# V kept per head pair as it lies in SBUF, its loads spread over SyncE's queue, and the last pair's transfers put in another order

## The chip, the cores and the metric

The kernel runs on one core of a Trainium2 chip: TensorE (PE), VectorE (DVE), ScalarE (ACT), GpSimd (POOL) and SyncE (SP), and 16 DMA engines that all of them feed. The metric is the device time of one execution in microseconds (us), the median of several runs; lower is better.

## The reference

One decoder layer in float32, 2048 tokens by 1024 features. One input projection feeds two branches; their gated, normed outputs are concatenated and go through one output projection, with a residual and a layer norm.

```python
# attention: 16 heads of 64, for each dilation in (1, 4, 16):
scores = einsum(q, k) + alibi            # keys: current and previous block of 128 on each
p = exp(scores - lse)                    # of the `dilation` residue subsequences
o[d] = einsum(p, v)
# the three dilations are merged by their log-sum-exp weights, gated by silu(z), RMS-normed
# Mamba-2 branch: causal conv, chunked state-space scan (chunks of 128), gate, RMS norm
u = concat(att, ssm)                     # 2048 features
out = layer_norm(alpha * x + u @ w_out)
```

## The kernel before

**Stage 1** (to about 1142 us) computes the input projection, the convolution and the scan, all in PE-bound blocks. Weights are split in two fp32r parts, and three matmuls stand for one product. V goes to a DRAM tensor `d_v[0]` in token order, 1024 features a token. `copy_v` then makes `d_v[1]`, the order that dilation 4 reads: 32 DRAM-to-DRAM transfers of 256 KB on POOL's queue, 16 in about 357 to 560 us and 16 in 864 to 1130 us, in pieces of 2 KB. In the second phase POOL's queue also reloads prepared weights (`w<-d_wc`, L237).

**Stage 2** (about 1142 to 1613 us) is attention, in 8 head pairs. A pair has 24 units, named (d, qd, half): d counts the dilations in the order 16, 4, 1, qd the four groups of blocks, half the head. PE runs a software pipeline: the scores of one unit (L947), the transposes of the unit two before (L976), the values of the unit three before (L1002). DVE adds bias and takes maxima (L953), ACT does the exps (L962), DVE copies the transposed probabilities out of PSUM (L978). For a unit, V is read through two tiles: `v`, and `vs`, which is V shifted by half a block.

What one pair leaves is merged during the next one: the softmax statistics are transposed (tile `st`, into `sT`), stored in `d_st`, gathered back in another order (`cm`, L1061), turned into weights in three steps (`weights`, on DVE, POOL and ACT), stored in `d_wd` and read back three times, once for each dilation, as a row broadcast over 64 partitions (`broadcast`, tile `wb`, L1089). `combine(0)` to `combine(5)` multiply (L1111), add (L1115) and gate them into the pair's u. u lies in a `wb` buffer until `keep_u` (L1096) stores it in `d_ua`; a broadcast starts with a memset of one column on DVE (L1087), which takes the buffer over. All pairs but the last one are merged on POOL; the last one on DVE.

**Stage 3** (about 1596 to 2002 us) is the output projection, in items of 24 matmuls (L1201 to L1203): block of tokens n, branch br (1 the scan, 0 attention), half of the features. The order is blocks 0 to 3 of the scan branch first (items 0 to 7), then block 0 of the attention branch (items 8 and 9), and so on. An item needs its block fetched (`fetch_raw`), split in two fp32r parts (`split`: cast L1167, subtraction L1169), its squares (L1174), and 8 weight tiles W[0..7] or W[8..15] (`load_w`, L1142). Item 8 is the first to need the last pair's u.

Code is written in the order of one list, and PE, DVE, ACT and POOL run in that order in stages 2 and 3. SP's queue was ordered by a scheduler in stage 3. Loads hang on the unit at which they are issued: `STEPS` gives the unit's combine step and a load on POOL's queue, `LOADS` the weight loads of the last pair. A queue issues in order: a transfer that has to wait holds up those behind it.

Of the kernel before, what the change touches and what calls it, by code (L numbers as in the profile page):

```python
# [17 lines left out]
D = 1024  # L18
NR = 16
# [9 lines left out]
def hybrid_layer(ctx, tc, xb, xc, w52, wv, wdt, convw, convb, dtb, alog, dskp, gcol, wout,  # L29
# [18 lines left out]
    d_v = [dtile(f"d_v{d}", [16, 128, D]) for d in range(2)]  # L48
# [10 lines left out]
    d_ua = dtile("d_ua", [16, 128, 7, 128])  # L59
# [11 lines left out]
    with ExitStack() as c1:  # L71
# [281 lines left out]
        def fin_v(s, p):  # L353
            def f(ci, q, b, e):
                for x in range(2):
                    nc.sync.dma_start(dap(d_v[0], 4 * (8 * p + 4 * q + 2 * b + x) * D + 512 * s + 256 * ci,
                                          [[64 * D, 32], [D, 4], [1, 256]]), e[:, 256 * x:256 * x + 256])
            return f
# [188 lines left out]
        def copy_v(s, b):  # L547

            o = (b % 4 * 512 + b // 4 * 16) * D + 512 * s
            nc.gpsimd.dma_start(dap(d_v[1], b * 128 * D + 512 * s, [[16 * D, 8], [D, 16], [1, 512]]),  # L550
                                dap(d_v[0], o, [[64 * D, 8], [D, 16], [1, 512]]))
# [298 lines left out]
    with ExitStack() as c2:  # L850
# [29 lines left out]
        def load_v(A, x, d, queue=nc.gpsimd):  # L880

            o, t, c0 = int(x == "vs"), io.tile([128, 16, 128], F32, name=x, bufs=3), A["pr"] * 128
            A[x][d] = t
            if d == 0:
                for j in range(4):
                    nc.gpsimd.dma_start(t[j:128:4], dap(d_v[0], j * D + c0, [[64 * D, 32], [4 * D, 16], [1, 128]]))
            else:
                queue.dma_start(t[:, 0:16 - o], dap(d_v[d % 2], 64 * o * D + c0,
                                                        [[D, 128], [128 * D, 16 - o], [1, 128]]))
# [193 lines left out]
        def broadcast(A, d):  # L1083

            wb = A["w", d] = cm_.tile([128, NR, NJ], F32, name="wb", bufs=3)
# [9 lines left out]
        def keep_u(A, queue):  # L1095
            queue.dma_start(dap(d_ua, A["pr"] * 128, [[7 * 128, 128], [128 * 7 * 128, 16], [1, 128]]),  # L1096
                            A["u"].rearrange("p (n t) -> p n t", t=128))

        def combine(A, k):
# [50 lines left out]
        def fetch_raw(n, br, u=None):  # L1150
# [5 lines left out]
            else:  # L1156
                queue.dma_start(u[:, 0:7], d_ua[n])
# [21 lines left out]
        def residual(n):  # L1179
            o = O[n] = os_[n // 2][:, n % 2 * D:n % 2 * D + D] if n < 4 else O.pop(n - 4)  # L1180
            (nc.scalar if n < 4 else nc.sync).dma_start(o, xc[n * 128:(n + 1) * 128, :])
# [38 lines left out]
        def norm(n):  # L1220
# [10 lines left out]
            if n == 15:  # L1231
                for s in (slice(0, 512), slice(512, D)):
# [13 lines left out]
                 (1, 1, 0): (1, "k", 1), (1, 2, 0): (2, "v", 1, 0), (1, 3, 0): (3, None, 0), (2, 0, 0): (None, "v", 1, 1),  # L1246
                 (2, 1, 0): (4, "vs", 1, 1), (2, 2, 0): (5, None, 0)}
        LOADS = {(1, 0, 0): ((8, None, "k_0"),), (1, 1, 0): ((9, None, "q_0"),), (1, 2, 0): ((11, None, "vs"),),
                 (1, 3, 0): ((12, 0, "q_1"), (13, 0, "v")), (2, 1, 0): ((10, None, "ex"),),
                 (2, 2, 0): ((14, 0, "v"), (15, 0, "vs"))}  # L1250
# [4 lines left out]
        with tc.manual_schedule(engines={E.PE, E.DVE, E.Activation, E.Pool, E.SP}):  # L1255
            for i in range(len(todo) + TA + 1):
# [27 lines left out]
                if i > TA:  # L1284
# [32 lines left out]
                    if pr == 7 and at in ((2, 0, 1), (2, 1, 0)):  # L1317
                        split(0, 1, slice(4 * qd, 4 * qd + 4), (0,))
                    if pr == 7 and at == (2, 1, 0):
                        split(0, 1, parts=(1,))  # L1320
# [11 lines left out]
                    if pr < 7:  # L1332
                        continue
                    for e, hf, name in LOADS.get(at, ()):
                        load_w(e, hf, name)
# [159 lines left out]
```

## Time and profile before

| what | value |
|---|---|
| runs | 2010.32, 2006.55, 2009.21 us; median 2009.21 |
| profiled execution | 2003.82 us, span 2002.0 us, clock 0.991 |
| busy: PE, DVE, ACT, POOL | 1945.7, 1275.8, 1120.0, 998.3 us |
| DMA | 447.67 MB, mean 224 GB/s |

The profile is one execution, 5.4 us under the median. PE is busy 97% of the span, so what is left to find lies in its few waits. "PE S L1203 <- DVE num L1169: 12.0, 1, 12.0" reads: PE, about to run line 1203 into tile S, waited for DVE's line 1169 on tile num, 12.0 us in total, once, 12.0 at the longest. An "issue" wait is one for which the profile shows no releaser.

### The profile page before, as it was taken

How to read it: one execution, taken by the hardware profiler on the slowest of the kernel's cores; microseconds unless marked ns; L12 is line 12 of the kernel's file. 1: busy time of each engine (PE TensorE's matmuls, PEld its weight loads, DVE VectorE, ACT ScalarE, POOL GpSimd, SP SyncE). 2: the span in 40 equal slices, each digit the busy share in tenths (PEclk: the TensorE clock that was granted, in tenths of full speed). 3: DMA queues.
4: the chain of work that ended last, by engine and by line, in shares of the span. 5: the costliest groups of instructions: out<-in, count | busy, mean ns of one | idle time of the engine just before them, and what ended most of it. 6: DMA issues, size and time to landing. Idle time of an engine off the chain costs nothing.

```text
span 2002.0 us, 42714 instructions
## 1 busy us (share of the span) xinstructions
PE 1945.7 (97%) x16008; PEld 1588.2 (79%) x16008; DVE 1275.8 (64%) x3204; ACT 1120.0 (56%) x3036; POOL 998.3 (50%) x877
## 2 busy tenths in 40 slices
PE   8999999999999999999999999999999888999998
PEld 7888899888888888988888877777777666888886
DVE  7655376887766655644454388888887736655553
ACT  5454343566556774456566488988888732322220
POOL 0366514666556667155565343676776622432221
PEclk9999999999999999999999999999999998999999
DMA  6788676566787876888888766888888988332210
GB/s 270 236 284 293 213 280 227 159 195 190 237 306 266 279 245 239 312 269 256 272 277 259 256 228 165 229 244 235 252 238 254 265 242 260 134 102 92 92 61 32
DMA packets 260656, 447.67 MB, mean 224 GB/s; under 512 B 44785, under 2 KB 146673, under 8 KB 249057
## 3 DMA queue, kind: packets, MB, share of 16 engines
q1 hardware_dynamic: 170912, 205.39, 32.2%
q0 software_dynamic: 39088, 142.54, 21.6%
q10 hardware_dynamic: 50448, 97.01, 15.7%
q8 instruction: 126, 2.06, 0.4%
q14 instruction: 82, 0.66, 0.1%
HBM read 301.85 MB, written 151.39 MB: 226 GB/s over the span
## 4 chain that ended last, share of the span: by engine, by line
PE 85%; DVE 5%; DMA 4%; ACT 3%; issue 2%; POOL 1%; SPq 0%; ACTq 0%; DVEq 0%; POOLq 0%
PE pp L260 13%; PE pp L264 13%; PE pp L262 13%; PE N L1002 7%; PE S L947 6%; PE T L976 5%; PE pp L309 4%; PE S L1201 4%; PE S L1203 4%; PE S L1202 3%; PE ss L309 2%; PE T L1201 2%; PE T L1203 2%; PE T L1202 2%; PE ss L627 2%
## 5 line engine op out<-in xcount | busy, mean ns | idle before, releaser
L217 POOL TENSOR_TENSOR w<-wr,w 128x512 fp32r<-128x512 f32 x217 | 285.6, 1327 | 268.2 <-ACT w L216 184.0
L962 ACT ACTIVATE P<-P,st 128x192 f32<-128x192 f32 (+1 forms) x768 | 323.4, 423 | 59.9 <-DVE st L953 55.4
L252 ACT COPY ev<-pp 128x512 f32<-128x512 f32 x200 | 117.1, 587 | 315.3 <-PE pp L264 281.5
L953 DVE CUSTOM_DVE_ANT_0 P<-S,tb 128x192 f32<-128x192 f32 (+1 forms) x768 | 205.8, 324 | 53.6 <-PE S L947 44.1
L272 DVE TENSOR_TENSOR ev<-pp,ev 128x512 f32<-128x512 f32 x152 | 101.2, 686 | 140.6 <-PE pp L264 95.9
L216 ACT CAST w<-wr 128x512 fp32r<-128x512 f32 x224 | 134.1, 620 | 23.5 <-DVE wr L211 11.9
L962 ACT ACTIVATION_READ_ACCUMULATOR P<-P,st 128x1 f32 x768 | 145.0, 189 | 0.0
L1111 POOL TENSOR_TENSOR wb<-num,wb 128x2048 f32<-128x2048 f32 x21 | 95.7, 4558 | 93.7 <-DMA wb<-d_wd 90.2
L978 DVE COPY PT<-T 128x512 f32<-128x512 f32 x192 | 131.7, 686 | 3.8 <-PE T L976 3.8
L976 PE MATMUL T<-ident,P 128*128 128x128 f32 x768 | 127.3, 288 | 6.7 <-DVE PT L978 4.5
L1002 PE MATMUL N<-PT,v 128*64 128x64 f32 (+1 forms) x1536 | 124.5, 259 | 4.2 <-DVE PT L978 3.5
L976 PEld LDWEIGHTS T<-ident,P 128*128 128x128 f32 x768 | 81.3, 141 | 52.9 <-ACT P L962 16.8
L211 DVE TENSOR_TENSOR wr<-wr 128x512 f32<-128x512 f32 x128 | 112.2, 877 | 9.3 <-DMA wr<-w 5.9
L947 PE MATMUL S<-k,ex 64*64 64x192 f32 (+1 forms) x2048 | 108.8, 322 | 3.2 <-issue 3.2
L1002 PEld LDWEIGHTS N<-PT,v 128*64 128x64 f32 x1536 | 79.4, 138 | 38.3 <-issue 22.7
L459 DVE SCALAR_TENSOR_TENSOR ss<-U,cw,ss 128x512 f32<-128x512 f32 x144 | 106.0, 752 | 2.9 <-ACT ss L455 0.6
L1177 DVE TENSOR_REDUCE tb<-P 128x128 f32<-128x1024 f32 x30 | 60.2, 2006 | 45.1 <-ACT P L1174 21.1
L1239 POOL TENSOR_TENSOR k<-k,wb 128x1024 f32<-128x1024 f32 x8 | 25.8, 3225 | 122.0 <-DVE k L1238 122.0
L587 ACT ACTIVATE mt<-csb,wdr 128x128 f32<-128x128 f32 x256 | 78.9, 395 | 0.9 <-PE ss L627 0.8
L947 PEld LDWEIGHTS S<-k,ex 64*64 64x64 f32 x2048 | 66.4, 134 | 15.4 <-issue 8.9
L596 DVE TENSOR_TENSOR mt<-mt,ss 128x1024 f32<-128x1024 f32 x32 | 39.0, 1220 | 54.1 <-ACT mt L592 53.7
L260 PE MATMUL pp<-TT4h,w 128*128 128x512 f32 x176 | 69.6, 395 | 0.0
(493 smaller groups left out, 5991.1 us busy)
## 6 DMA issues: line engine op xcount, KB each, us to landing
wr<-w ACTq DMA_DIRECT2D x164, 256.0 KB
d_wc<-w SPq DMA_DIRECT2D x48, 512.0 KB
w<-d_wc POOLq DMA_DIRECT2D x48, 512.0 KB, 6.4
wb<-d_wd SPq DMA_DIRECT2D x48, 512.0 KB
d_wo<-wot POOLq DMA_DIRECT2D x32, 512.0 KB, 4.3
csb<-d_cs ACTq DMA_DIRECT2D x32, 512.0 KB
d_wv<-w SPq DMA_DIRECT2D x14, 1024.0 KB
w<-d_wv POOLq DMA_DIRECT2D x14, 1024.0 KB, 8.7
```

Source lines behind the costliest of these rows:

```text
L216: nc.scalar.copy(h, r)
L217: low.tensor_tensor(l, r, h.bitcast(F32), op=OP.subtract)
L260: nc.tensor.matmul(ps, w[:, 0, k], th[:, k], start=start and k == 0, stop=False, skip_group_check=not start)
L262: nc.tensor.matmul(ps, w[:, 0, k], tl[:, k], start=False, stop=False, skip_group_check=not start)
L264: nc.tensor.matmul(ps, w[:, 1, k], th[:, k], start=False, stop=(k == 3), skip_group_check=not start)
L309: nc.tensor.matmul(o, (th, tl)[j == 1][:, k, t], w[:, int(j == 2), k], start=start and r % 2 == k == j == 0, stop=(k == 3 and j == 2), ski ...
L947: nc.tensor.matmul(o, A["q"][d][64 * h:64 * h + 64, blk, 64 * a:64 * a + 64], kv, start=True, stop=True)
L953: nc.vector.tensor_tensor_reduce(P[:, h, cs], sp[h][:, cs], t, -0.125, 3.0e38, OP.add, OP.min, accum_out=stat(A, 0, d, h, blk))
L962: nc.scalar.activation(p, p, AF.Exp, bias=stat(A, 0, d, h, blk), scale=-1.0, accum_out=stat(A, 1, d, h, blk))
L976: nc.tensor.transpose(tp[:, h, i], P[:, h, 256 * i:256 * i + 128], ident)
L978: nc.vector.tensor_copy(pt, tp)
L1002: nc.tensor.matmul(o, l, r, start=start, stop=True, skip_group_check=True)
```

## The change

1. *V's layout.* `d_v[1]` goes. `d_vt[1]` and `d_vt[2]` hold V for dilations 4 and 1 by head pair, each as the [128, 2048] tile that SBUF takes. `copy_v` issues two transfers where it issued one, in pieces of 512 B. A load of `v` is then 128 rows of 8 KB, one of `vs` two halves of 64 rows of 7.5 KB.
2. *Where loads are issued.* `v` and `vs` of dilation 4 move from POOL's queue to SP's, at (0,0,0) and, for the next pair, (2,0,1); `v` of dilation 1 at (0,1,1) and `vs` at (1,1,1), where both were at (0,0,0). `keep_u` moves from (1,0,0) to (0,0,1), and writes rows of 8 KB; `fetch_raw` of the attention branch now reads 7 pieces of 512 B for each partition.
3. *The last pair and the passage to stage 3.* The fetch of blocks 0 and 1 of the scan branch, the loads of W[10], W[11], W[14], W[15] and of z for pair 7, and `split(0, 1)` stand at other units. After item 0 SP gets: weights' store, broadcast 0, two residuals, broadcasts 1 and 2, `keep_u` of pair 6, two residuals, all in program order. ACT's queue carries no transfers there any more. At item 2 only `combine(0)` stands, at item 3 the third block's `split`, then `combine(1)` to `combine(5)`.

The core of the diff:

```diff
+            nc.gpsimd.dma_start(dap(d_vt[1], t + n * 512, [[128, 4], [16 * 2048, 8], [2048, 16], [1, 128]]),
+                                dap(d_v, 16 * n * D + c, [[512 * D, 4], [64 * D, 8], [D, 16], [1, 128]]))
+            nc.gpsimd.dma_start(dap(d_vt[2], t + 32 * n * 2048, [[2048, 32], [128, 16], [1, 128]]),
+                                dap(d_v, 32 * n * D + c, [[D, 32], [128 * D, 16], [1, 128]]))
...
-                queue.dma_start(t[:, 0:16 - o], dap(d_v[d % 2], 64 * o * D + c0,
-                                                        [[D, 128], [128 * D, 16 - o], [1, 128]]))
+                queue.dma_start(t[0:64, 0:15], d_vt[d][A["pr"], 64:128, 0:15])
+                queue.dma_start(t[64:128, 0:15], d_vt[d][A["pr"], 0:64, 1:16])
...
-            queue.dma_start(dap(d_ua, A["pr"] * 128, [[7 * 128, 128], [128 * 7 * 128, 16], [1, 128]]),
-                            A["u"].rearrange("p (n t) -> p n t", t=128))
+            queue.dma_start(d_ua[A["pr"]], A["u"])
...
-                if last:
-                    broadcast(A, d)
...
-                 (1, 1, 0): (1, "k", 1), (1, 2, 0): (2, "v", 1, 0), (1, 3, 0): (3, None, 0), (2, 0, 0): (None, "v", 1, 1),
-                 (2, 1, 0): (4, "vs", 1, 1), (2, 2, 0): (5, None, 0)}
...
+                 (1, 1, 0): (1, "k", 1), (1, 2, 0): (2, None, 0), (1, 3, 0): (3, None, 0), (2, 0, 0): (None, "v", 1, 0),
+                 (2, 1, 0): (4, None, 0), (2, 2, 0): (5, None, 0)}
...
+                 (1, 3, 0): ((12, 0, "q_1"), (13, 0, "v")), (2, 0, 0): ((11, None, "num"), (14, 0, "v"), (15, 0, "vs")),
+                 (2, 1, 0): ((10, None, "ex"),)}
...
+                    if at == (0, 0, 0) and pr:
+                        load_v(pairs[pr], "v", 1, nc.sync)
+                    if at == (0, 1, 1) and pr:
                         load_v(pairs[pr], "v", 2, nc.sync)
-                        load_v(pairs[pr], "vs", 2, nc.sync)
-                    if pr > 1 and at == (1, 0, 0):
+                    if pr > 1 and at == (0, 0, 1):
                         keep_u(pairs[pr - 2], nc.sync)
+                    if pr and at == (1, 1, 1):
+                        load_v(pairs[pr], "vs", 2, nc.sync)
+                    if pr < 7 and at == (2, 0, 1):
+                        load_v(pairs[pr + 1], "vs", 1, nc.sync)
...
                 if i == 2:
-                    for j in range(2):
-                        scaled(j)
-                    add(*adds.pop(0))
-                    add(*adds.pop(0))
-                    for j in range(3):
-                        combine(A, j)
+                    combine(A, 0)
                     load_w(0, 0, "num")
...
+                        broadcast(A, 0)
                         for n in range(2):
                             residual(n)
+                        broadcast(A, 1)
+                        broadcast(A, 2)
+                        keep_u(pairs[6], nc.sync)
+                        for n in range(2, 4):
+                            residual(n)
```

SP's queue around the merge of one pair in a steady pair, before: `d_st` and `cm` are the statistics' store and gather, the two loads named d_v are V's for the pair itself, `d_wd` the weights' store, `wb<-d_wd` a broadcast (x2, one for each head), `d_ua` u's store, `tb` a table.

```order
L1055 DMA d_st_115<-sT 16x16x8 x4
L1061 DMA cm<-d_st_115 128x6x32
L888 DMA v<-d_v_84 128x16x128
L888 DMA vs<-d_v_84 128x15x128
L878 DMA tb_15636<-tabs 128x2x320
L1081 DMA d_wd_123<-cm 128x3x32
L1089 DMA wb<-d_wd_123 64x2048 x2
L1096 DMA d_ua<-wb 128x16x128
```

And the same place after:

```order
L1061 DMA d_st_115<-sT 16x16x8 x4
L1067 DMA cm<-d_st_115 128x6x32
L892 DMA v<-d_vt_85 128x2048
L1103 DMA d_ua<-wb 128x2048
L892 DMA v<-d_vt_86 128x2048
L882 DMA tb_14582<-tabs 128x2x320
L1087 DMA d_wd_123<-cm 128x3x32
L1096 DMA wb<-d_wd_123 64x2048 x4
L894 DMA vs<-d_vt_86 64x1920
L895 DMA vs<-d_vt_86 64x1920
```

u's store now stands ahead of the weights' store and the broadcasts, and the load of vs behind two of the broadcasts.

DVE in the passage to stage 3, before, from the products of the first items on: L1111 and L1115 are the last pair's combine, L1169 and L1177 split and square sums of the third block (then of others), L1218 adds an item's result.

```order
L1218 SCALAR_TENSOR_TENSOR k<-S,st,k 128x512 x2
L1111 TENSOR_TENSOR wb<-num,wb 128x2048 x2
L1115 TENSOR_TENSOR wb<-wb 128x2048
L1169 TENSOR_TENSOR num<-P,num 128x1024
L1177 TENSOR_REDUCE tb_19949<-P 128x128
L1111 TENSOR_TENSOR wb<-num,wb 128x2048
```

And after:

```order
L1115 TENSOR_TENSOR wb<-num,wb 128x2048
L1173 TENSOR_TENSOR vs<-P,vs 128x1024
L1222 SCALAR_TENSOR_TENSOR k<-S,st,k 128x512 x2
L1115 TENSOR_TENSOR wb<-num,wb 128x2048
L1119 TENSOR_TENSOR wb<-wb 128x2048
L1181 TENSOR_REDUCE tb_20003<-P 128x128
```

The third block's subtraction stands behind one combine step, where it stood behind three.

PE at the end of attention, before: L1002 are values, L1201 to L1203 the product of item 0, whose weight tiles are k (W[8]), q (W[9]), ex (W[10]) and so on.

```order
L1002 MATMUL N_19728<-PC,v 64x64 x2
L1002 MATMUL N_19727<-PT,v 64x64 x2
L1002 MATMUL N_19727<-PT,vs 64x64 x2
L1002 MATMUL N_19728<-PT,vs 64x64 x2
L1002 MATMUL N_19728<-PT,v 64x64 x2
L1201 MATMUL S<-ex,num 128x512
L1202 MATMUL S<-ex,num 128x512
```

And after, where the whole product stands ahead of the last units' values (L1008):

```order
L1008 MATMUL N_19715<-PC,v 64x64 x2
L982 MATMUL T<-ident,P 128x128 x4
L1207 MATMUL S<-q,vs 128x512
L1205 MATMUL S<-ex,vs 128x512
L1206 MATMUL S<-ex,vs 128x512
L1207 MATMUL S<-ex,vs 128x512
L1205 MATMUL S<-num,vs 128x512
```

The product's matmuls from ex (W10) on moved from behind these values to ahead of the last two units' values and the transpose of st.

More of the change, by code (lines that the diff above doesn't have):

```diff
@@ L47, in hybrid_layer @@
     d_za = [dtile(f"d_za{i}", [128, S]) for i in range(8)]
-    d_v = [dtile(f"d_v{d}", [16, 128, D]) for d in range(2)]
+    d_v = dtile("d_v", [16, 128, D])
+    d_vt = {d: dtile(f"d_vt{d}", [8, 128, 16, 128]) for d in (1, 2)}
     d_wc = dtile("d_wc", [12, 7, 128, 1024])
@@ L1083, in broadcast @@
         def broadcast(A, d):
-            wb = A["w", d] = cm_.tile([128, NR, NJ], F32, name="wb", bufs=3)
+            pool, name = (io, "v") if A["pr"] == 7 and d == 2 else (cm_, "wb")
+            wb = A["w", d] = pool.tile([128, NR, NJ], F32, name=name, bufs=3)
             if d and A["pr"] < 7:
@@ L1316, in hybrid_layer @@
                         load_z(pairs[pr - 1])
[L1317 to L1320, printed above, removed]
+                    if pr < 7 and at == (2, 0, 1):
+                        load_v(pairs[pr + 1], "vs", 1, nc.sync)
+                    if pr == 7:
+                        if at == (1, 0, 0):
+                            X = big("ex", F32)
+                            for j in range(2):
+                                fetch_raw(j, 1, X[:, j * D:j * D + D])
+                        if at == (1, 2, 0):
+                            free.append(big("vs"))
+                        if at == (2, 0, 0):
+                            zt7 = cm_.tile([128, NR, NJ], F32, name="num", bufs=6)
+                            nc.sync.dma_start(f2(zt7), d_za[7])
+                        for e, hf, name in LOADS.get(at, ()):
+                            load_w(e, hf, name)
+                        if at == (2, 0, 0):
+                            free.append(big("num"))
+                        if at in ((1, 2, 1), (1, 3, 0)):
+                            split(0, 1, slice(4 - 4 * half, 8 - 4 * half), (0,))
+                        if at == (2, 0, 0):
+                            split(0, 1, parts=(1,))
+                        if at in ((2, 2, 1), (2, 3, 0)):
+                            fetch_raw(qd, 1)
                     if at in STEPS:
@@ L1331, in hybrid_layer @@
                         permute(pairs[pr + 1], 1)
[L1332 to L1335, printed above, removed]
-                    if at == (2, 0, 0):
-                        zt7 = cm_.tile([128, NR, NJ], F32, name="num", bufs=6)
-                        free += [big("num"), big("num")]
-                    if at == (1, 2, 0):
-                        X = big("ex", F32)
-                        for j in range(2):
-                            fetch_raw(j, 1, X[:, j * D:j * D + D])
-        with tc.manual_schedule(engines={E.PE, E.DVE, E.Activation, E.Pool}):
+        with tc.manual_schedule(engines={E.PE, E.DVE, E.Activation, E.Pool, E.SP}):
             A = pairs[7]
@@ L1347, in hybrid_layer @@
             free.append(big("ex"))
-            fetch_raw(2, 1)
             squares(0, 1)
@@ L1386, in hybrid_layer @@
                         os_.insert(0, big("k_1", F32))
+                        broadcast(A, 0)
                         for n in range(2):
                             residual(n)
+                        broadcast(A, 1)
[3 more added lines that the diff above has]
+                            residual(n)
+                    if i == 3:
+                        for n in range(2):
+                            scaled(n)
+                        add(*adds.pop(0))
+                        add(*adds.pop(0))
+                        combine(A, 1)
+                        load_w(1, 0, "num")
+                        combine(A, 2)
                     squares(*ops[j])
-                    if i == 0:
-                        keep_u(pairs[6], nc.scalar)
-                        nc.scalar.dma_start(f2(zt7), d_za[7])
                     for m in (j + 2,) if 4 < j < 30 else ():
@@ L1406, in hybrid_layer @@
                 if i == 4:
-                    for e, name in enumerate(("num", "vs", "v", "wb", "num", "wb", "num")):
-                        load_w(1 + e, 0, name)
+                    for e, name in enumerate(("wb", "wb", "num", "wb", "num")):
+                        load_w(3 + e, 0, name)
                         if e == 2:
```

32 lines of the change are left out of this document (14 added, 18 removed).

## The prediction

> **What bounds the kernel now.** I read the page first, then a table of stretches, then the waits of PE, and then, where PE waits, the chain and the timelines around it.
>
> ```profile
> PE 1945.7 (97%) x16008; PEld 1588.2 (79%) x16008; DVE 1275.8 (64%) x3204; ACT 1120.0 (56%) x3036; POOL 998.3 (50%) x877
> ```
>
> The span is 2002.0 us, so PE stands still for 56 us in all: no edit that leaves PE's own instructions alone can bring more than that, plus what a slow clock costs. The next table (columns: window, its length, then PE, PEld, DVE, ACT, POOL busy, clock, DMA share, GB/s) says where those 56 us lie.
>
> ```profile
> 860.00:1140.00 280.00, 280.00 (x1574) 233.40 (x1573) 131.54 (x247) 163.64 (x336) 157.34 (x165) 1.00 0.82 264
> ...
> 1180.00:1540.00 360.00, 346.48 (x6653) 260.21 (x6651) 302.11 (x1531) 309.74 (x1384) 229.71 (x184) 1.00 0.79 224
> 1540.00:1590.00 50.00, 47.24 (x900) 35.14 (x900) 41.48 (x213) 42.83 (x195) 32.41 (x27) 1.00 0.85 233
> 1590.00:1613.00 23.00, 18.28 (x278) 13.46 (x268) 14.80 (x37) 11.30 (x35) 21.58 (x11) 0.78 0.87 296
> 1613.00:1660.00 47.00, 33.79 (x158) 26.97 (x151) 15.12 (x19) 10.92 (x16) 8.36 (x12) 0.91 0.97 249
> 1660.00:1700.00 40.00, 39.09 (x160) 31.04 (x160) 27.52 (x33) 9.53 (x13) 7.85 (x11) 0.93 0.86 272
> ```
>
> Stage 1, where V is copied, is bound by PE without a gap (the first row is the second half of the copies). Attention idles 13.5 us (360.00 less 346.48) in 1180 to 1540, 2.8 in the first part of pair 7, and the passage into the output projection idles 4.7 and then 13.2 us, at a clock of 0.78 and 0.91. Those are the places that the change touches. PE's waits from 1180 to 1700 name what is late:
>
> ```profile
> PE S L1203 <- DVE num L1169: 12.0, 1, 12.0
> PE T L976 <- DVE PT L978: 4.5, 4, 1.7
> PE S L947 <- issue: 3.5, 4, 1.4
> PE N L1002 <- DVE PT L978: 3.5, 3, 1.7
> PE S L1203 <- POOL num L1169: 3.2, 1, 3.2
> ```
>
> And DVE, which PE waits for, is itself held by transfers (1140 to 1700):
>
> ```profile
> DVE wb L1111 <- DMA wb<-d_wd: 13.9, 2, 9.2
> ...
> DVE wb L1087 <- DMA d_ua<-wb: 9.4, 4, 2.6
> ...
> DVE mm L1069 <- DMA cm<-d_st: 3.7, 5, 1.3
> ```
>
> The second row is a memset of one column (it claims broadcast 2's buffer), standing in DVE's program order until the store of an older u has left that buffer; the third is the weights step waiting for the gather of the softmax statistics. Both hold up the score work behind them, and their 13.1 us of DVE become the 8.0 us that PE waits for L978.
>
> **The change, part by part.**
>
> *V's layout, stage 1.* Each copy becomes two (32 more issues of 256 KB), in pieces of 512 B where one was in pieces of 2 KB.
>
> ```profile
> L550 POOL DMA_DIRECT2D d_v<-d_v x32: 622/647/671, 357.2 to 1129.6; - x32
> L237 POOL DMA_DIRECT2D w<-d_wc x48: 537/574/600, 842.4 to 1134.6; - x48
> ...
> DMA to landing us min/median/max: 3.9/6.4/9.9
> ```
>
> 32 x 0.65 = 21 us more on POOL, which is busy 157 of 280 us in the second phase of the copies, so it has room. 8.4 MB more, at the 310 GB/s that a full queue gives below, is 27 us of all engines over some 480 us: the share rises by about 0.06, to 0.88 in the second phase. What shares POOL's queue and could suffer are the weight reloads (second row; the third is their landing): nobody waits for any now, and the slowest landing is 3.5 us above the median, so that much delay is covered. Cost 0; ends -0.5 and, if some cover goes, +5; beyond that is a rival.
>
> *V's loads, pairs 1 to 7.* Rows around pair 4's start, from SP's timeline and POOL's (start, us, what):
>
> ```profile
> 1384.36 0.38 SPq L1061 DMA_DIRECT2D cm<-d_st  x1
> 1384.79 0.54 SPq L888 DMA_DIRECT2D v<-d_v  x1
> ...
> 1395.32 1.13 SPq L1089 DMA_DIRECT2D wb<-d_wd  x2
> 1396.50 0.59 SPq L1096 DMA_DIRECT2D d_ua<-wb  x1
> 1397.20 5.82 SPq L1089 DMA_DIRECT2D wb<-d_wd  x2
> ```
>
> ```profile
> 1377.29 1.21 POOL L888 DMA_DIRECT2D vs<-d_v  x1
> ```
>
> POOL's 512 B load of vs was issued at 1377.29, while SP was storing and gathering the statistics. Now that load goes to SP some eight units earlier, in the pair before, so nothing large is issued beside the gather; SP issues it ahead of this pair's first V load, as before. Between gather and broadcasts stand two loads of V and u's store (3 MB) where two loads of V stood. Of the 3.7 us that DVE waits for the gather I expect nearly all to go.
>
> *keep_u.* It was issued at 1396.50, between two broadcasts, and the memset waited for its landing. Now it is issued seven units earlier (a unit is 2.2 us, so 15 us), behind one load of V, and by the memset it has been done for some 10 us: the 9.4 us go. What is late next: vs of the widest dilation, now behind broadcasts 0 and 1.
>
> ```profile
> 1386.00:1393.00 7.00, 5.85 (x87) 3.96 (x84) 6.00 (x32) 4.96 (x24) 3.71 (x9) 1.00 1.07 310
> 1396.50:1401.00 4.50, 4.50 (x101) 3.45 (x94) 4.17 (x22) 4.12 (x19) 0.00 (x0) 1.00 1.06 226
> ...
> 1586.00:1590.00 4.00, 3.28 (x74) 2.60 (x74) 3.09 (x14) 3.09 (x15) 3.98 (x3) 1.00 1.09 381
> ```
>
> At full share the old V loads ran at 310 GB/s, broadcasts at 226, the output projection's long rows at 381. From 1396.5, two broadcasts of 1 MB at 226 take 9.2 us and vs 2.8 more, with 1 to 2 for issue and landing: 1409.5 to 1410.5, against a first use at about 1411.4 in this pair (seventeen units and values three units behind). A slack of one or two: I charge 1 us over all pairs. [...]
>
> Sum for 1180 to 1540: 8.0 for L978, 2 of the other 5.5 (waits called issue, at moments of full DMA share), less 1: -9 to -10. I take -10. Ends: -13.5 (all idle gone) and -3 (vs late each pair).
>
> *Pair 7 and the passage.* Rows of the chain, then of SP, PE, ACT and DVE:
>
> ```profile
> 1597.86 2.36 POOL num L1169
> ```
>
> ```profile
> 1613.11 0.30 PE L1041 MATMUL T<-ident,st 128*64 128x128 f32 x1
> ...
> 1624.60 0.38 SPq L1081 DMA_DIRECT2D d_wd<-cm  x1
> 1633.60 9.47 SPq L1089 DMA_DIRECT2D wb<-d_wd  x6
> 1624.80 8.36 ACTq L1392 DMA_DIRECT2D num<-d_za  x1
> ...
> 1646.81 2.29 DVE L1111 TENSOR_TENSOR wb<-num,wb 128x2048 f32<-128x2048 f32 x1 [9.23 <-DMA wb<-d_wd]
> 1653.74 2.29 DVE L1111 TENSOR_TENSOR wb<-num,wb 128x2048 f32<-128x2048 f32 x1 [4.64 <-DMA wb<-d_wd]
> ...
> 1658.28 1.22 DVE L1169 TENSOR_TENSOR num<-P,num 128x1024 fp32r<-128x1024 f32 x1
> ...
> 1662.54 2.27 DVE L1111 TENSOR_TENSOR wb<-num,wb 128x2048 f32<-128x2048 f32 x1
> ...
> 1672.04 1.23 DVE L1169 TENSOR_TENSOR num<-P,num 128x1024 fp32r<-128x1024 f32 x1 [1.16 <-ACT num L1167]
> ```
>
> ```profile
> v<-d_wo POOLq DMA_DIRECT2D x4, 512.0 KB, 7.1
> ...
> ex<-d_wo POOLq DMA_DIRECT2D x1, 1024.0 KB, 5.1
> ```
>
> Before, with the statistics' transpose at 1613.1 (call it st): store of the weights st+11.5, broadcasts issued only st+20.5 (that store took 9 us, beside u's store and zt on ACT's queue), products with them at st+33.7 and +40.6, then the third block's split at +45.2: this is the 12.0 us. Item 8 (first item of the attention branch) could start at +60.
>
> Now: split(0,1)'s casts stand two units sooner, but POOL's half of it still stands behind combine(3) and two weight loads, at about the same place (1600 of the old time). W10, which the first product needs third, is issued after it, at about 1601, and lands 5 to 9 later by these rows (its own 5.1 before, and some room for company), 1606 to 1610. PE now has that whole product ahead of the last two units' values and the st transpose: 18 matmuls of 0.22 to 0.43 us and 4 us of attention behind them. So st' is st+4 to +7; I take +6. From there: weights stored at st'+11.5; the store, with ACT's two transfers out of its way, 4 us; broadcast 0 (1 MB at 226 GB/s, and 2 for issue and landing) at +23; combine(0) to +25.3, the split's subtraction, now right behind it, to +26.5. PE has items 1 to 5 after st' (5 x 5.33 = 26.7), so the 12.0 us go. Next late: 1 MB of residuals and broadcast 1 land at +31, broadcast 2 at +36.5, and the tail of combine with the first attention split took 11 us (1662.54 to 1673.3): item 8 at +47.4. PE has done items 6 and 7 at +37.3, so it waits some 10 us there, and the clock dips again after it. Net: st'+47.4 = st+53.4 against st+60, -6.6. The estimate leans on transfers I haven't seen, so I take -5. Ends: -20 (no wait at item 8, and the dips of 1613 to 1700, about 6 us of clock, gone) and +4 (W10 at the end of its spread, the store slow as before).
>
> Sum: 0 - 10 - 5 = -15, on the profiled execution's 2003.8, which lies 5.4 below the median of the runs, 2009.2. Against the median that is 1994.
>
> **The rivals.**
> - *vs arrives late.* If every pair waits 1 us or so for vs (broadcasts slower than 226 GB/s beside the q load), pairs give -4: 2000. For it: the slack of one or two us; against: V's other loads and u's store are over before the first broadcast is issued. [...]
> - *The passage gains nothing:* W10 late, or the store of the weights slow again: 1999.
> - *All of it goes:* pairs -13.5, the passage -15 or more: 1980. Against it: the waits called issue, and the chain of broadcasts still ahead of item 8.
> - *The copies cost more (slower):* 16 copies more on POOL's queue in 864 to 1130, in 512 B pieces, ahead of weight reloads. It decides once a reload lands over 3.5 us late; then PE stops at the next block of weights. 16 x 1.5 us = 24, less 15 gained: 2018. For it: the share of 0.82 there; against: POOL's free time and no wait now.
> - *The change doesn't do what it says:* the buffer of broadcast 2 was held by something else as well (combine's own reader on POOL); the stall stays, and the passage alone gives 2004.
>
> **How the numbers follow.** Forecast 0.48 (1988 to 2000 its own range); vs late 0.13; passage nothing 0.10; all gone 0.12; copies cost 0.10; stall stays 0.07. A measurement here tells 0.2% (4 us) from no change. Faster than 2005: 0.79; within: 0.11 (half of the stall case, weaker forms of the first two and of the copies); slower: 0.10. The range, 1980 to 2011, leaves out most of the copies' case and half of the best one.
>
> **What would show it.** The memset's wait for d_ua and the wait for cm gone from DVE's waits in pairs 2 to 6; PE's 1180 to 1540 idle near 4 us; no DVE or PE wait for vs. In the passage: the split of the third block without PE wait, a new PE wait of about 10 us some 37 us after the transpose of st, and a wait for W10 before it. PE still without a gap in 860 to 1140. I am wrong if PE gaps appear at weight reloads, if a row of PE waits names v or vs, or if item 8 starts later than 60 us after st.

## The result and the profile after

The changed kernel takes 2061.37 us (four runs, 2057.52 to 2064.93) against 2008.66 us for the kernel before: ratio 1.0263, 95% interval 1.0241 to 1.0284. It is slower by 2.6%, where 0.7% faster was forecast, and outside the range. Its profiled execution has a span of 2058.8 us, 56.8 more than before. PE's own row of the page splits that at once:

```profile
PE 1968.0 (96%) x16008; PEld 1602.4 (78%) x16008; DVE 1288.1 (63%) x3204; ACT 1120.3 (54%) x3036; POOL 1020.2 (50%) x897
```

The same 16008 matmuls are 22.3 us longer busy, and PE stands still for 90.8 us instead of 56.3. The two belong together. The traces' clock records grant half speed for 36 us of the span before and for 81 us of the changed kernel's, and 45 us more at half speed are those 22 us. In the changed kernel eight such stretches lie between 1150 and 1600 us, and each begins within 2 us of the end of a stop of PE. Windows of the changed kernel (columns as in the prediction) show both:

```profile
340.00:600.00 260.00, 256.77 (x1129) 211.50 (x1128) 209.90 (x278) 149.41 (x262) 174.42 (x174) 0.99 0.75 223
860.00:1140.00 280.00, 277.04 (x1561) 230.46 (x1560) 131.68 (x249) 166.99 (x344) 174.93 (x178) 1.00 0.87 275
...
1300.00:1420.00 120.00, 108.18 (x1960) 81.14 (x1956) 86.80 (x442) 89.40 (x400) 73.84 (x54) 0.93 0.79 209
1420.00:1540.00 120.00, 106.17 (x1983) 79.58 (x1972) 88.81 (x452) 92.22 (x411) 74.79 (x57) 0.97 0.80 217
```

Stage 1 is no longer without gaps, and the pairs idle 13.8 us of every 120 in the last row, at a clock of 0.97. PE's waits over the whole run are of other kinds than before:

```profile
PE N L1008 <- issue: 19.9, 10, 3.5
PE S L953 <- issue: 10.4, 5, 2.8
PE N L1008 <- DMA vs<-d_vt: 10.2, 1, 10.2
...
PE S L1205 <- ACT num L1171: 5.8, 1, 5.8
PE pp L261 <- ACT ev L253: 3.2, 3, 1.9
...
PE T L982 <- ACT P L968: 3.0, 1, 3.0
PE pp L261 <- DMA w<-d_wc: 3.0, 2, 1.7
...
PE T L982 <- issue: 2.7, 1, 2.7
```

The 12.0 us before item 6 and the waits for DVE's copy are gone, as forecast. In their place stands "issue", 34.5 us over the whole run; between 1150 and 1600 us it is 33.3, against 5.1 before. PE runs the same matmuls in the same order up to the passage, so the time of each stretch can be read between the same two matmuls of each trace (us, worked out from their start times; pair 0 is left out, as it takes 58.3 in every one of them; e1 to e14 are experiments, told below):

| stretch | before | changed | e1 | e5 | e6 | e8 | e11 | e14 |
|---|---|---|---|---|---|---|---|---|
| stage 1, to pair 0 | 1149.8 | 1158.7 | 1146.7 | 1147.1 | 1146.1 | 1180.6 | 1147.7 | 1147.9 |
| pairs 1 to 6 | 336.1 | 376.1 | 348.1 | 371.0 | 346.2 | 353.2 | 353.4 | 337.9 |
| pair 7, to item 0 | 54.7 | 63.3 | 61.4 | 62.8 | 62.3 | 60.9 | 53.8 | 58.3 |
| item 0 to item 8 | 73.1 | 67.6 | 67.9 | 69.8 | 68.1 | 68.1 | 70.0 | 69.9 |
| item 8 to the end | 319.4 | 324.4 | 323.4 | 323.3 | 321.5 | 324.9 | 320.4 | 320.7 |
| "issue" waits of PE, 1150 to 1600 | 5.1 | 33.3 | 17.6 | 29.7 | 14.2 | 17.9 | 20.5 | 8.1 |

Pairs 1 to 6 lose 40 us, stage 1 loses 9, pair 7 loses 8.6; the passage to item 8 gains 5.5, and 5 are lost after it.

Each column is one execution. Kernels whose code is the same up to the passage differ in the pairs by 7.1 us (e11 and e12), 2.2 (e13 and e15) and 0.6 (e14 and e17), and the execution shown of the kernel before lies 5 us under its median. A few us in these rows therefore mean little. The 73.1 us of the kernel before in the passage are such a case: five runs that leave the order of work there as it was (e3, e11, e13, e14, e16) take 69.9 to 71.2, so against them the change gains only some 2 to 4 us.

**What an "issue" wait is here.** PE's timeline of the changed kernel, in pair 4, at two of them (start, us, what, and the idle time ahead):

```profile
1436.58 0.40 PE L1008 MATMUL N<-PT,vs 128*64 128x64 f32 x7
1439.02 0.22 PE L1008 MATMUL N<-PT,vs 128*64 128x64 f32 x1 [2.05 <-issue]
...
1444.46 0.22 PE L1008 MATMUL N<-PC,v 64*64 64x64 f32 x1
1448.13 0.27 PE L1008 MATMUL N<-PC,v 64*64 64x64 f32 x1 [3.46 <-issue]
```

PE stops inside a group, between two matmuls with the same operands, so no data is late. The stops of the pairs stand at matmuls 9820, 9947, 10200, 10833, 10961, 11214, 11847, 11974 and so on: multiples of 126.7 apart. And each of the fifteen "issue" waits of over 1 us between 1150 and 1600 ends 1.2 to 1.7 us after the end of a packet of 16 KB on the queue that the profile's page calls "instruction". So does the wait of 3.0 us that the view puts down to ACT (P L968). The queue's line:

```profile
q8 instruction: 126, 2.06, 0.4%
```

Here 1436.14 to 1437.49 and 1445.30 to 1446.54. There are 126 such packets for 16008 matmuls. I read them as PE's own instructions, fetched block by block (a refill is the fetch of one block): PE stops where the next block hasn't come. The counts agree: 16008 matmuls in 126 packets are 127 for each, as many as lie between the nearest two stops (9820 and 9947). By this reading the refills cost the kernel before little, 5.1 us of "issue" between 1150 and 1600, and this one 33.3. Counted from PE's start of the block before, the packet starts later than 5 us in 3 of 59 blocks of stage 2 before and in 15 of 59 after; most blocks last 5 to 9 us, so a packet that late can come too late. What it waits behind isn't in the records; the experiments look for it.

**The passage.** SP's queue in pair 7, PE's transpose of st, and DVE around item 8, in the changed kernel:

```profile
1618.56 1.10 SPq L1096 DMA_DIRECT2D wb<-d_wd  x2
1619.70 2.10 SPq L1159 DMA_DIRECT2D ex<-d_us  x4
1621.90 1.09 SPq L1096 DMA_DIRECT2D wb<-d_wd  x2
1623.67 0.45 SPq L894 DMA_DIRECT2D vs<-d_vt  x1
```

```profile
1676.84 0.30 PE L1047 MATMUL T<-ident,st 128*64 128x128 f32 x1
...
1699.40 2.29 DVE L1115 TENSOR_TENSOR wb<-num,wb 128x2048 f32<-128x2048 f32 x1 [9.00 <-DMA wb<-d_wd]
1701.61 1.22 DVE L1173 TENSOR_TENSOR vs<-P,vs 128x1024 fp32r<-128x1024 f32 x1
...
1725.36 1.23 DVE L1173 TENSOR_TENSOR num<-P,num 128x1024 fp32r<-128x1024 f32 x1 [1.15 <-ACT num L1171]
```

Here st' is the start of that transpose, as in the prediction. From it on, the forecast holds to some 2 us: combine(0) at st'+22.6 (forecast 23), item 8's split from st'+48.5 (its end forecast at 47.4); PE waits 5.8 us there (forecast 10). Counted from item 0, st' also comes 6.2 us later than before (19.0 against 12.8), as forecast. But item 0 itself is late: vs stood in SP's queue behind two broadcasts and the fetch of X (the scan branch's blocks, `ex<-d_us`), and PE waited 10.2 us for it.

### The profile page after: what moved, and what is told of

Same layout as the page of the kernel before. It is cut to its first block, busy times and chain, and to the rows that moved or that the text cites. A ratio compares the mean times of both kernels' runs of the same rounds, so it can differ in the third digit from the quotient of the medians.

```text
span 2058.8 us, 42766 instructions
## 1 busy us (share of the span) xinstructions
PE 1968.0 (96%) x16008; PEld 1602.4 (78%) x16008; DVE 1288.1 (63%) x3204; ACT 1120.3 (54%) x3036; POOL 1020.2 (50%) x897
## 4 chain that ended last, share of the span: by engine, by line
PE 62%; DMA 5%; issue 4%; DVE 2%; POOL 2%; ACT 1%; SPq 0%; ACTq 0%; POOLq 0%; DVEq 0%
PE N L1008 8%; PE pp L261 8%; PE pp L265 7%; PE pp L263 7%; PE S L953 6%; PE T L982 5%; PE S L1205 3%; PE S L1207 3%; PE S L1206 3%; PE ss L631 1%; PE T L1205 1%; PE T L1206 1%; PE T L1207 1%; PE ss L622 1%; PE T L990 1%
## 5 line engine op out<-in xcount | busy, mean ns | idle before, releaser
L968 ACT ACTIVATE P<-P,st 128x192 f32<-128x192 f32 (+1 forms) x768 | 322.1, 421 | 89.1 <-DVE st L959 83.9
L1115 POOL TENSOR_TENSOR wb<-num,wb 128x2048 f32<-128x2048 f32 x21 | 95.4, 4543 | 108.2 <-DMA wb<-d_wd 90.1
L968 ACT ACTIVATION_READ_ACCUMULATOR P<-P,st 128x1 f32 x768 | 144.0, 188 | 0.0
L984 DVE COPY PT<-T 128x512 f32<-128x512 f32 x192 | 131.8, 686 | 10.0 <-PE T L982 9.9
L1008 PE MATMUL N<-PT,v 128*64 128x64 f32 (+1 forms) x1536 | 126.9, 262 | 5.0 <-ACT num L1039 3.1
L212 DVE TENSOR_TENSOR wr<-wr 128x512 f32<-128x512 f32 x128 | 118.6, 927 | 8.3 <-DMA wr<-w 4.9
L953 PE MATMUL S<-k,ex 64*64 64x192 f32 (+1 forms) x2048 | 113.5, 331 | 7.9 <-issue 7.9
L1008 PEld LDWEIGHTS N<-PT,v 128*64 128x64 f32 x1536 | 81.3, 140 | 41.1 <-issue 26.6
L1243 POOL TENSOR_TENSOR k<-k,v 128x1024 f32<-128x1024 f32 x8 | 25.8, 3221 | 123.2 <-DVE k L1242 123.2
L261 PE MATMUL pp<-TT3h,w 128*128 128x512 f32 x176 | 70.5, 401 | 6.2 <-ACT ev L253 3.2
```

The source lines that it names most:

```text
L212: tt = lambda o, a, b, op=OP.subtract: nc.vector.tensor_tensor(q[o], q[a], q[b], op=op)
L261: nc.tensor.matmul(ps, w[:, 0, k], th[:, k], start=start and k == 0, stop=False, skip_group_check=not start)
L953: nc.tensor.matmul(o, A["q"][d][64 * h:64 * h + 64, blk, 64 * a:64 * a + 64], kv, start=True, stop=True)
L968: nc.scalar.activation(p, p, AF.Exp, bias=stat(A, 0, d, h, blk), scale=-1.0, accum_out=stat(A, 1, d, h, blk))
L984: nc.vector.tensor_copy(pt, tp)
L1008: nc.tensor.matmul(o, l, r, start=start, stop=True, skip_group_check=True)
```

## The experiments

Short names e1 to e18; "pairs" is the row "pairs 1 to 6" of the table, worked out in the same way, and "issue" its last row. All ratios are to the kernel before, run beside, with their 95% intervals.

**e1 to e4: layout or places?** e1 takes the changed kernel and gives V its old layout and single copies back (its loads stay at their new places on SP). e2 keeps the new layout but pads it, so that loads move in pieces of 512 B. e3 puts the new layout into the kernel before. e4 is e2 with u in its old layout.

```diff
# e2
-    d_vt = {d: dtile(f"d_vt{d}", [8, 128, 16, 128]) for d in (1, 2)}
+    d_vt = {d: dtile(f"d_vt{d}", [8, 128, 16, 192]) for d in (1, 2)}
...
-                queue.dma_start(t, d_vt[d][A["pr"]])
+                queue.dma_start(t, d_vt[d][A["pr"], :, :, 0:128])
```

> The changed kernel with V's old layout (one copy for dilation 4, loads in pieces of 512 B) but all of its new places in the queues. Theory A (PE's own instruction refills, 16 KB each on queue 8, wait on the DMA engines behind rows of 8 KB, and PE stands still at every second block of 127 matmuls): PE's waits called issue fall from 34.5 us to under 12, PE's clock is back near 0.99, and with stage 1's 9 us gone too the time is 2000 to 2020. Rival B (the new places pile up more bytes at once, whatever the pieces): issue waits stay over 25 us and only stage 1's 9 us come back: about 2050.

> The changed kernel with V's rows padded in DRAM, so that the same loads at the same places, with the same doubled copies, move in pieces of 512 B instead of 8 KB. A: issue waits fall to under 15 us, stage 1's 9 us stay, 2015 to 2030. B: as the changed kernel, 2055 to 2062. If the doubled copies themselves made the refills late, 2055 to 2062 too.

> The kernel before with V's new layout and the doubled copies alone; every load, u's store and the last pair stay where they were. A: issue waits rise from 6 to over 18 us and stage 1 loses 9: 2035 to 2055. B: only stage 1's 9 us: about 2017.

> As the kernel with V's rows padded, and u stored and fetched in its old layout (pieces of 512 B) at the new place. A: u's 8 KB rows are a small part (1 MB of 6 a pair): within 6 us of the kernel with padded V alone, on the faster side. B: no difference to the changed kernel.

Measured: e1 2018.16 us (1.0062, interval 1.0045 to 1.0078); e2 2055.51 (1.0246); e3 2031.69 (1.0128, 1.0113 to 1.0143); e4 2050.07 (1.0235). The change without V's layout costs 10.9 us (e1) and the layout alone 24.5 (e3); together they cost 52.7, so they don't simply add. The layout carries most of the loss, but the size of the pieces does not: e2's loads are pieces of 512 B, and its pairs (376.4) and "issue" waits (33.8) are those of the changed kernel. Theory A, that rows of 8 KB are what the refills wait behind, falls. In e3, with the loads and u's store in their old places, "issue" is only 7.1 and the loss takes another form; its DVE waits have

```profile
DVE wb L1093 <- DMA d_ua<-wb: 22.5, 5, 5.3
```

where the kernel before had 9.4: the store lands later, and PE waits 15.5 us for L984, DVE's copy, behind it.

**e5, e6, e8: the halves.** What e1 and e2 still differ in is that e2 loads vs as two transfers of 64 partitions. The trace's packet records (SP's queue, 1225 to 1590 us) pointed at them: a row of 7.5 KB of vs takes 0.55 us in the changed kernel. e5 is e1 with vs in two halves and nothing else; e6 is the changed kernel with V in token order inside a pair, so that vs is one transfer; e8 adds shifted rows in DRAM, so that vs is one transfer of whole rows.

```diff
# e5, against e1
-                queue.dma_start(t[:, 0:16 - o], dap(d_v[d % 2], 64 * o * D + c0,
-                                                    [[D, 128], [128 * D, 16 - o], [1, 128]]))
+                for h in range(1 + o):
+                    m = 128 - 64 * o
+                    queue.dma_start(t[64 * h:64 * h + m, 0:16 - o],
+                                    dap(d_v[d % 2], 64 * (o + h) * D + c0, [[D, m], [128 * D, 16 - o], [1, 128]]))
# e6, against the changed kernel (and copy_v to match)
+                queue.dma_start(t[:, 0:16 - o], dap(d_vt[d], A["pr"] * 128 * 2048 + 64 * o * 128,
+                                                    [[128, 128], [128 * 128, 16 - o], [1, 128]]))
```

> The kernel with the old layout of V and the new places, with one thing more: vs is loaded as two transfers of 64 partitions, in the same pieces of 512 B. Theory C (a transfer into 64 partitions runs at half the rate: 0.55 us for a row of 7.5 KB of vs, where whole rows of 8 KB into 128 partitions take 0.31; it then fills the DMA engines and PE's refills come late): pairs 1 to 6 take 360 to 376 us instead of 348, total 2030 to 2046. Rival D (reading one pair's V from one compact megabyte is what is slow, not the halves): pairs stay at 348, total 2018.

> The changed kernel with V still copied twice and kept per pair, but in token order inside the pair, so that vs is one transfer of 128 partitions in pieces of 512 B. C: pairs 1 to 6 fall from 376 to 345 to 355 us, stage 1 keeps its 9 to 15 us, total 2022 to 2034. D: pairs stay at 370 to 380, total 2050 to 2060.

> The changed kernel with a third, shifted copy of V's rows in DRAM, so that vs is one transfer of 128 partitions in whole rows of 7.5 KB. More copies in stage 1 (it may lose 15 to 25 us there; only the pairs are read). C: pairs 1 to 6 take 340 to 355 us, rows of vs about 0.31 us each. If long rows as such make the refills late, or D holds: 370 or more.

Measured: e5 2046.39 us (1.0191, 1.0168 to 1.0214), e6 2016.39 (1.0047, 1.0032 to 1.0062), e8 2058.81 (1.0261; 31 us of it in stage 1, with more copies). The pairs of e5 go from e1's 348.1 to 371.0 by the halves alone; from the changed kernel's 376.1 those of e6 come back to 346.2, of e8 to 353.2. PE's waits of e5, then of e6 (1150 to 1600):

```profile
PE N L1005 <- issue: 15.0, 9, 2.3
PE S L950 <- issue: 10.6, 6, 2.8
```

```profile
PE N L1007 <- issue: 7.9, 7, 2.2
PE S L952 <- issue: 5.8, 5, 2.2
```

And the packets themselves: of the pieces of 512 B on SP's queue 3 to 6% take over 0.045 us where vs is one transfer (before, e1, e6), 23 and 25% where it is two (e2, e5); the usual piece takes 0.027, those 0.054. Rows of 7.5 KB take 0.552 in halves, 0.334 as one transfer (e8). These are means; the medians are 0.572 and 0.291. So in these runs a transfer into half of the partitions runs at about half the rate, 0.572 us a row against 0.291 by the medians. Theory C stands, D falls. What in the hardware makes it so, no run shows.

**Stage 1.** e6 copies V twice too, and against its expectation loses nothing in stage 1 (1146.1). The number of copies is thus not what costs. The copies of the two kernels differ in where the pieces of 512 B land. In the changed kernel those of the first copy (L552) land at steps of 8 KB and those of the second (L554) in one run of 256 KB; in e6 the first lands in one run and the second at steps of 64 KB. POOL's groups in 340 to 600, changed kernel, then e6:

```profile
L552 POOL DMA_DIRECT2D d_vt<-d_v x16 | 19.2, 1197 | 0.4 <-issue 0.4
L554 POOL DMA_DIRECT2D d_vt<-d_v x16 | 11.5, 718 | 0.0
```

```profile
L554 POOL DMA_DIRECT2D d_vt<-d_v x16 | 10.7, 672 | 0.0
L552 POOL DMA_DIRECT2D d_vt<-d_v x16 | 10.4, 649 | 0.0
```

Only the changed kernel's L552 is slow to issue, so scattered writing alone, which e6's L554 has too, isn't what makes it slow. The packet records show one thing more: on POOL's queue the changed kernel has 3072 packets of 32 B in this window, 192 for each issue of L552, and e6 has none. Why that copy alone has them stays open. Median landing of both copies was 7.0 us against 4.2 in e6 (3.9 before). In the changed kernel ACT then waits up to 6.1 us for a store of the convolution (`d_xs<-co`), and PE for ACT; 5.3 of the 9 us are lost between 472 and 500 us, where this stands. The rest is lost in the second half of the copies, where PE waits twice for reloaded weights (`PE pp L261 <- DMA w<-d_wc`, above): the slowest reload lands in 12.6 us, against 9.9 before. That it is landing and not POOL's time was not tried apart.

**e7, e9, e10: where vs stands, and broadcasts on two queues.** e7 is e1 with vs between broadcasts 0 and 1; e9 is e6 with vs right behind v, ahead of the weights' store; e10 is e9 with the second half of every broadcast on POOL's queue.

> Old layout and new places, with the load of vs for the widest dilation moved between broadcasts 0 and 1 (which puts it ahead of the last pair's fetch of X as well). If two broadcasts back to back make the refills late (they too go to 64 partitions each) and vs comes too late only in pair 7: issue waits fall from 17 to under 10 us, pairs to 336 to 344, the 10.9 us wait for vs goes, total 1998 to 2008. If not: 2015 to 2020.

> The kernel with V in token order inside a pair (copied twice, each load one transfer of 128 partitions), and the load of vs for the widest dilation back in front of the weights' store, right behind v. If what is left of the loss in the pairs is vs's megabyte lying among the broadcasts, pairs 1 to 6 fall from 346 to 330 to 340 us and issue waits from 14 to under 9; pair 7's 11.9 us wait for vs goes. Total 1990 to 2000, under the kernel before. If the rest of the loss is u's store or the loads moved from POOL's queue: pairs stay at 346, total 2003 to 2008.

> As the kernel with vs early, and the second half of each broadcast (64 partitions of rows of 8 KB) issued on POOL's queue instead of SP's, so that two halves are in flight together. [...]

The vs of "the widest dilation" in these texts and in the prediction is that of dilation 1, the last one of a pair.

Measured: e7 2027.23 us (1.0105), pairs 351.3, "issue" 19.2: 9 us slower than e1, where a gain was hoped for. e9 2016.15 (1.0048, 1.0030 to 1.0065), pairs 341.5, "issue" 11.0: 4.7 us less than e6 in the pairs, where 6 to 16 were hoped for, and pair 7 and the passage took it back, since POOL's half of split(0,1) now comes 8.3 us late. e10 2058.93 (1.0258): PE waits 23.1 us for `v<-d_v`, since POOL's queue stands waiting for the weights' store with V's loads behind it; whether the rows of two halves in flight together go faster, it doesn't show.

**e11, e12: the prediction's two main terms, each alone in the kernel before.** e11 moves only u's store; e12 also moves the third block's split on DVE.

```diff
# e11
-                    if pr > 1 and at == (1, 0, 0):
+                    if pr > 1 and at == (0, 0, 1):
                         keep_u(pairs[pr - 2], nc.sync)
```

> The kernel before with one line changed: u's store seven units earlier, as in the change, its pieces of 512 B kept. If the prediction's term for it was right, the memset's wait on DVE (9.4 us) goes and with it most of the 8.0 us that PE waits for DVE: pairs 1 to 6 at 328 to 332 us instead of 336, total 2000 to 2004. If the store between broadcasts 0 and 1 also kept PE's refills from coming late (two broadcasts now stand back to back), issue waits rise from 5 to 10 or more and the gain is eaten: 2005 to 2012.

> The same, and on DVE in the passage the third block's split right behind combine(0), as in the change; the last pair's loads and SP's order stay as before. The 12.0 us wait of PE before item 6 falls to under 2, and part comes back at item 8, which still needs the third broadcast: passage to item 8 66 to 70 us instead of 73.1, total 3 to 6 us under the kernel with the early store alone. If broadcast 0 is as late as before (1646), the split cannot stand before 1649 and PE waits 2 us.

Measured: e11 2014.09 us (1.0032, 1.0018 to 1.0046); e12 2009.21 (1.0016, 1.0003 to 1.0029). In e11 the memset's wait is gone from DVE's rows, and yet the pairs are longer: 353.4 against 336.1. These 17 us are the difference of two single executions; e12, whose code is the same up to the passage, has 346.3, and by the medians of the whole kernel e11 is 7.0 us slower. PE's waits of e11 (1150 to 1600):

```profile
PE N L1002 <- issue: 10.5, 10, 2.6
PE S L947 <- issue: 8.9, 5, 3.2
...
PE N L1002 <- DVE PT L978: 0.3, 1, 0.3
```

The waits for DVE, 8.0 us, became 0.3 (2.1 in e12), and "issue" went from 5.1 to 20.5 (17.2 in e12). With u's store gone from between them, broadcasts 0 and 1, 64 partitions each time, are issued back to back. That this is the cause isn't shown: in e7 a megabyte of vs stands between them again, and "issue" is 19.2.

In e12 PE's wait of 12.0 us (10.8 in e11) is gone, but in its passage (1590 to 1700) stand three others:

```profile
PE S L1201 <- ACT num L1167: 3.3, 1, 3.3
PE S L1201 <- DVE k L1218: 3.2, 1, 3.2
...
PE N L1209 <- DVE tb L1177: 2.2, 1, 2.2
```

These are the cast for item 8, an item's result that DVE now adds later, and the square sums. So e12's passage is 68.3, as expected, but against e11's 70.0 that is 1.7 us; the same edit on top of e14 (e17) makes it longer, 71.8 against 69.9. The sooner split alone is worth nothing clear.

**e13 to e18: what the refills wait behind.** e13 is e11 with broadcasts in pieces of 2 KB; e14 is e11 with each broadcast as four transfers of 32 partitions, in turn to the lower and the upper half; e15 is e12 with e13's pieces, e16 the kernel before with them, e17 is e12 with e14's quarters, e18 is e12 with eighths of 16 partitions.

```diff
# e14
-            for h in range(2):
-                nc.sync.dma_start(f2(wb[64 * h:64 * h + 64]), dap(d_wd[A["pr"]], (d * 2 + h) * S, [[0, 64], [1, S]]))
+            for g in (0, 2, 1, 3):
+                h = g // 2
+                nc.sync.dma_start(f2(wb[32 * g:32 * g + 32]), dap(d_wd[A["pr"]], (d * 2 + h) * S, [[0, 32], [1, S]]))
```

> The kernel with u's store early and nothing else, and the broadcasts read in pieces of 2 KB instead of rows of 8 KB (the weights' rows are padded in DRAM; their store becomes three transfers). If 8 KB rows on the engines are what makes PE's refills late: issue waits fall from 21 to under 9 us, pairs 1 to 6 from 353 to 326 to 334, total 1992 to 2000. If it is the bytes queued, or the half rate into 64 partitions: pairs stay at 350 to 356, total 2012 to 2018.

> The same kernel with early store, rows of 8 KB, but each broadcast issued as four transfers of 32 partitions, in turn into the lower and the upper half. If the half rate into 64 partitions is the cause and engines overlap neighbouring transfers: mean of the 8 KB rows on SP's queue falls from 0.55 to under 0.45 us, pairs to 335 to 345. If not: both unchanged, total 2012 to 2018.

> The kernel with u's store early and the split sooner, and the broadcasts in pieces of 2 KB. By the first theory: pairs 326 to 334, passage 68, total 1986 to 1996, under the kernel before. By the others: about 2009, as without the pieces.

> The kernel before with the broadcasts in pieces of 2 KB and nothing else. By the first theory the few late refills (5 us of issue waits) go, and the memset still waits: total 2000 to 2006. By the others: 2005 to 2010.

> The kernel before with u's store early, the split sooner on DVE in the passage, and broadcasts as four transfers of 32 partitions in turn into the lower and the upper half. If the two gains add: pairs 336 to 340, passage 67 to 69, total 1994 to 2000, ratio under 0.996. If the passage loses what the split gains: 2001 to 2005.

> The same with broadcasts as eight transfers of 16 partitions, one row for each engine. If a refill waits behind what one transfer has on an engine: issue waits in the pairs fall below those with quarters, to under 6 us, pairs 328 to 336; SP's issue grows by 2 us a broadcast, which may cost some of it. If the quarters helped by something else: pairs 336 to 342, or worse by SP's issue.

In the table, the last column is the mean of all packets of 8 KB on SP's queue (1225 to 1590 us), the loads of z into 128 partitions among them.

| | us | ratio (interval) | pairs | "issue" | 8 KB row, us |
|---|---|---|---|---|---|
| e11 | 2014.09 | 1.0032 (1.0018 to 1.0046) | 353.4 | 20.5 | 0.546 |
| e13 | 2014.26 | 1.0033 (1.0022 to 1.0044) | 347.3 | 18.4 | in pieces |
| e14 | 2002.78 | 0.9969 (0.9958 to 0.9979) | 337.9 | 8.1 | 0.517 |
| e15 | 2012.91 | 1.0018 (1.0008 to 1.0029) | 345.1 | 13.0 | in pieces |
| e16 | 2012.15 | 1.0017 (1.0006 to 1.0027) | 348.2 | 13.2 | in pieces |
| e17 | 2003.53 | 0.9984 (0.9972 to 0.9996) | 338.5 | 10.4 | 0.518 |
| e18 | 2056.80 | 1.0244 (1.0222 to 1.0266) | 381.0 | 17.2 | 0.709 |

Smaller pieces don't help (e13, e15, e16), as with V. In e18 a row takes 0.71 us, and SP needs 11.3 us to issue the sixteen transfers of two broadcasts, where e14's eight took 4.8. Which of the two holds the broadcasts up wasn't told apart. PE then waits for k, whose load stands on POOL's queue behind a combine step that waits for the broadcasts:

```profile
PE S L947 <- DMA k<-d_k: 20.1, 5, 7.1
PE N L1002 <- issue: 11.7, 8, 3.0
```

e14 is faster than both kernels (0.31% under the kernel before, 6 us), and e17 agrees in the pairs. That e14's pairs are no shorter than the 336.1 of the kernel before probably comes of that single execution, as said under the first table; against e11 and e12 they are 8 to 15 us shorter. PE's waits of e14:

```profile
PE N L1002 <- DVE PT L978: 6.6, 5, 2.0
PE N L1002 <- issue: 3.7, 4, 1.6
...
PE S L947 <- issue: 2.4, 4, 1.0
```

But its rows are hardly faster (0.517 against 0.546), so quarters don't help by the rate. In the trace of before the first 16 rows of a broadcast start within 0.35 us (1396.62 to 1396.97), and the 17th (1397.44) when the first of them ends. If that is one row on each of the 16 DMA engines, quarters halve what one transfer puts on each (two rows in place of four); one row each, in e18, should then have been better still, and the slow broadcasts of e18 spoil that test. Why quarters bring the refills back in time stays open, and quarters alone, with u's store in its old place, weren't tried. The waits for L978 are back with a DVE wait of 8.0 us for the gather (`cm<-d_st`; 0.4 in e11).

## Why the prediction was wrong

Of its three signs of being wrong, two came: PE waited for reloaded weights (3.0 us) and for vs (10.2 us). Item 8 came 48.6 us after the transpose, not later than 60.

- *V's layout, stage 1 (term 0, upper end +5): mis-sized.* It cost 9.0. The new issue was priced at the old one's 0.65 us; L552 took 1.20, and landing 7.0 instead of 3.9. A delay of 3.5 us was called covered, but with the slowest reload only 2.7 us later than before PE already waited. The number of copies, which the slower rival was built on with 1.5 us for each that no row gives, costs nothing in e6; how L552 writes does.
- *V's loads: failed, and this is the largest part.* vs was priced at 2.8 us, by the 381 GB/s of the output projection's long rows, a transfer of another width. It ran at about half the rate of a whole transfer (0.55 us a row of 7.5 KB, against 0.33 in e8), though the broadcasts, 64 partitions too and at 226 GB/s, stood in the same fence. e5 against e1: 23 us in the pairs, 28 by the medians of the whole kernel.
- *keep_u (9.4 us go): right in the mechanism, wrong in the sum.* The wait went; e11 shows that moving the store makes the kernel 7.0 us slower by the medians (17 in the pairs of the one execution), where 8 us were to be gained. The step that failed is "what is late next": it named vs, and what came late, as the packets of 16 KB are read here, were PE's instructions ("issue" 20.5 us in e11 against 5.1).
- *The waits called issue, taken as 2 us to be gained:* they became the largest loss. They were left as moments "of full DMA share", without asking what PE waits for in them. In the trace of before all seven of them ended 1.3 to 1.5 us after the end of a 16 KB packet on queue 8.
- *vs late, the first rival:* it named the place, at the wrong price; it happened in pair 7 alone, once, 10.2 us, where X's fetch stands ahead of it as well.
- *The passage:* right from item 0 on (st' 6.2 us later, item 8's split at 48.5 against 47.4, the 12.0 us gone), wrong ahead of item 0 by the wait for vs. That the row gains 5.5 where 5 were forecast is in part luck: against the five runs with the old order it gains 2 to 4, and the sooner split alone gained nothing clear (e12, e17).
- *The clock:* no term had it. 22.3 us of the 56.8 are the same matmuls at a lower clock, most of it in the stretches that have the stops.

The loss thus has two known parts in the pairs, the halves (e5: 23 us) and the new places on SP's queue (e1: 12 us; that much of it is of e11's kind is a guess), one in stage 1 and one in pair 7. Some 5 of the 40 us in the pairs are left over. Of the 5 us after item 8 some 3.4 are clock, by 6.8 us at half speed that the kernel before doesn't have there; the rest wasn't traced.

## What to carry to other kernels

Before a transfer is split by partitions, count how many partitions each piece reaches: here half the partitions meant about half the rate (a row of 7.5 KB took 0.55 us against 0.33; of the pieces of 512 B about a quarter took 0.054 us in place of 0.027), and a layout that needs no split (e6) brought the pairs from 376.1 back to 346.2 us. Read the "issue" waits of the engine that bounds: here the long ones stood at multiples of 126.7 matmuls and 1.2 to 1.7 us behind packets of the instruction queue, and with transfers moved they rose from 5.1 to 17.6 (e1) and 20.5 us (e11), even though no data was late. Removing a stall on a helper engine also moves transfers, and here that lost more than the stall had cost (e11: 8.0 us of PE's waits became 0.3, and the kernel took 7.0 us more); try it alone before building on it. And read a stretch from more than one execution where a few us decide.

## What the runs showed of the hardware

- On the queue called "instruction" 126 packets of 16 KB stood for 16008 matmuls, in the same DMA records as data, and the long "issue" waits of the changed kernel lay multiples of 126.7 matmuls apart. In stage 2 the packets started up to 6.7 us after PE began the block before (changed kernel; 9.2 in e11), and PE stopped for 1 to 3.5 us at a time. It went on 1.2 to 1.7 us after the packet's end.
- The granted clock fell to half for 3.4 or 6.8 us at the end of eight of the fifteen "issue" waits of over 1 us in the changed kernel (1150 to 1600 us).
- Mean time of a row of 7.5 KB: 0.33 us in a transfer into 128 partitions (e8), 0.55 into 64 (changed kernel). Mean of all rows of 8 KB on SP's queue, with broadcasts into 64 partitions 0.55 (e11), 32 in turn to both halves 0.52 (e14), 16 in turn 0.71 (e18).
- A DRAM-to-DRAM copy of 256 KB in pieces of 512 B took POOL 1.20 us to issue where 192 packets of 32 B came with it (pieces at steps of 8 KB, L552 of the changed kernel), and 0.65 to 0.72 us where none came, in one run or at steps of 64 KB alike (e6, and L554).
